# Four groups of small float32 matrix products taken in two halves of 64 weight columns

## The chip, the cores and the metric

The kernel runs on one core of a Trainium2 chip. A core has a matrix engine (TensorE, in the profile PE for its products and PEld for its weight loads), three engines for work on tiles (VectorE or DVE, ScalarE or ACT, GpSimd or POOL) and a queue processor, SyncE or SP, from which most transfers are issued. Matrix products read SBUF and write PSUM, which has eight banks. The metric is the device time of one execution in microseconds; the median of three runs before the change is 2164.58 us.

## The reference

One decoder layer over 4096 tokens of width 1024. The input is normalised and modulated to h; one projection of h feeds three groups of heads side by side. Their outputs are gated, joined, projected, normalised and added to the input.

```python
def _gla_mixer(h, q, k, v, gk1, gk2, gk_b, norm_w):
    gk = jax.nn.log_sigmoid(((h @ gk1) @ gk2 + gk_b).astype(f32)) / GLA_GATE_NORMALIZER
    ...
    def step(S, inp):
        b = jnp.cumsum(g_c, axis=2)
        A = jnp.einsum('bhid,bhjd,bhijd->bhij', q_c, k_c, jnp.exp(diff))
        o = A @ v_c + jnp.einsum('bhid,bhdv->bhiv', q_c * jnp.exp(b), S)
        S = ...
# in _rwkv7_mixer
    a = jax.nn.sigmoid((a0 + (xa @ a1) @ a2).astype(f32))
```

The groups are attention over a window of 128 tokens (8 heads), RWKV-7 (4 heads, a recurrence over tokens with a 64 by 64 state per head) and GLA (4 heads with 32 keys and 64 values each). The change touches four small products: the gate `(h @ gk1) @ gk2 + gk_b` of GLA, the scores `A` of GLA, the output `o` of GLA (scores by values plus queries by state), and `(xa @ a1) @ a2` of RWKV, called a-lora here.

## The kernel before

The work has two halves. The first goes through 16 steps of 256 tokens and computes h, its transpose (written to DRAM), the projections that RWKV and GLA need, and both recurrences, whose outputs go to DRAM. The second half does attention, the gates and the output projection. The change lies in the first half; the second half's program text is the same.

**Products and their shapes.** Large projections are float16 products with 128 by 128 weights and 256 moving columns. Small products are float32. A product with fewer than 128 weight rows or columns uses a part of the matrix engine: the code calls the pair (row quarters, column quarters) its mode. RWKV's products are already written for halves: `atp`, `rp`, `up` and one `yp` in mode (2, 2), that is 64 rows by 64 columns, `sp` and the other `yp` in mode (4, 2), 128 rows by 64 columns; parts of its triangular solve (`Xp`, `Xq`) have 32 by 32. The column half of a product is given by the PSUM partitions that it writes, 0 to 63 or 64 to 127.

**The stages of a step.** Each stage is a generator, and step i has eleven: among them `stage_a` (h and its transpose, `tp`), `stage_p` (projections `pv`, `lp`, `zz`, `gqk`), `stage_d` (the stream "w": GLA gate, decays, a-lora), `stage_r` (GLA), `stage_qa`, `stage_qb`, `stage_qc` (scores and triangular solve of RWKV, with a way through DRAM), `stage_k`, `stage_v` and `stage_q2` (the RWKV recurrence). The four groups of products are:

- `gp` in `gla_gate`, called from `stage_d`: 17 rows, 128 weight columns, 128 moving columns, twice per step. ACT (`ga`) and DVE (`gl`) read it.
- `aps` in `stage_d`: rows 64 to 127, 128 weight columns, 256 moving, twice per step; ACT (`ta`) reads it.
- `gap` in `stage_r`: for each of two blocks of 128 tokens (`a`) and each half of the heads (`hp`), 64 rows, 128 weight columns, 256 moving. The two halves lie in two PSUM banks, "at" and "mq". DVE masks them into `qb`.
- `op_` in `stage_r`: for each block, `qg` by the state `Gc` (128 rows, 128 weight columns, 256 moving), then per head the masked scores `qb` by values (64 moving columns), all summed in bank "at". ACT copies it to `osb`.

"at" has one buffer and is shared with `atp` of `stage_qa`; "mq" is shared by many.

**What sets the order.** The order of the instructions on each engine is not that of the program text. A first pass (`emit`, `Lane`) steps the generators by estimated times; there a float32 product counts 4 passes of its moving columns, and 0.55 of that if it writes at most 64 partitions. This gives each instruction a rank. A second pass (`Order.note`, `Order.pin`) lists every instruction with estimated durations, what it needs and which buffers it waits for, and then schedules all five engines, SP's and POOL's included, greedily by rank and fixes the order found. For PE it keeps a mode: a change of mode waits for the array to empty and costs 0.094 us in the estimate. While PE is in full mode (4, 4), a ready product of another mode is put off as long as full ones are ready, up to `TILING_WAIT`, 0.6 us; while PE is in another mode it goes on with that mode as long as anything of it is ready:

```python
if e == "PE" and mode is not None and steps[k].array[0] != mode:
    same = [q for q in at if steps[q].array[0] == mode]
    wait = max(now - ready[e][q] for q in at if steps[q].array[0] != mode)
    if same and (mode != (4, 4) or wait < TILING_WAIT):
        k = same[0]
```

The estimate of a float32 product's issue is 0.007 us a pass in mode (4, 4), 0.009 with one row quarter, 0.16 in mode (2, 4), 0.03 otherwise; its length is two passes of two cycles per moving column, at least 0.109 us a pass if it uses all columns.

The profile's line L320 is the helper that records every instruction, so groups are told apart by tile names.

Of the kernel before, what the change touches and what calls it, by code (L numbers as in the profile page):

```python
# [21 lines left out]
P = 128  # L22
D = 1024
T = 4096
NT = 256
# [358 lines left out]
def hybrid_kernel(ctx, tc, x, vecs, rows, adaw, w1, wl, w2, wo, w2aug, a2, gk2, cst, ctr, ctg, abias, out):  # L384
# [5 lines left out]
    PE = Lane(model, nc.tensor, *LANES[3], serial=True)  # L390
# [189 lines left out]
    def gla_gate(vg, zlT, ga, gl, tile_of):  # L580
        zp = tile_of("zp")
        for a in range(2):
            PE.transpose(zp[:17, a * P : (a + 1) * P], vg[:, a, 256:273], ident)
        V.tensor_copy(zlT, zp[:17, :NT])
        yield [zlT, "m"]
        gp = tile_of("gp")
        for a in range(2):
            PE.matmul(gp[:, a * P : (a + 1) * P], zlT[:, a * P : (a + 1) * P], gk2s, start=True, stop=True)
        S.activation(ga, gp[:, :NT], AF.Abs)
        S.activation(ga, ga, AF.Exp, scale=-1.0)  # L590
        S.activation(ga, ga, AF.Ln, bias=1.0)
        V.scalar_tensor_tensor(gl, gp[:, :NT], 0.0, ga, op0=ALU.min, op1=ALU.subtract)
# [31 lines left out]
    with ExitStack() as p1:  # L624
# [18 lines left out]
        def cs2(shape, name, dt=F32):  # L643
            return wt(shape, name, 2, dt, "c2")
# [36 lines left out]
        a2s = pp.tile([P, 256], F32, name="a2s")  # L681
        nc.scalar.dma_start(a2s[64:128, :], a2)
        gk2s = cp.tile([17, 128], F32, name="gk2s")
# [92 lines left out]
        for n, cc in enumerate((4, 5, 0, 6, 7, 1, 2, 3)):  # L776
            if cc in PE_BLOCKS:
                for jj in range(2):
                    aw = half_tile().rearrange("p (k c) -> p k c", k=KD)
                    SP.dma_start(aw, adaw[cc, :, :, jj * P : (jj + 1) * P])  # L780
                    for k in range(KD):
                        PE.matmul(adp[:, 2 * cc + jj : 2 * cc + jj + 1], aw[:, k, :], scol[:, k : k + 1], start=(k == 0),
                                  stop=(k == KD - 1))
# [25 lines left out]
        hp = mt("hp")  # L809
# [292 lines left out]
        def stage_d(i):  # L1102

            e = E[i]
            yield [("vg", i), ("w", i - 1)]
            vg = e["vg"]
            yield [vg, "m"]
            gl = wt([P, NT], "gl", 1)
            yield from gla_gate(vg, b1([17, NT], "zlT"), b1([P, NT], "ga"), gl, mt)
            yield [gl, "m"]  # L1110
            cgp = mt("cgp")
            for a in range(2):
                PE.matmul(cgp[:, a * 129 : (a + 1) * 129], gl[:, a * P : (a + 1) * P], CTG, start=True, stop=True)
            egp = wt([P, 2, 129], "egp", 2)
            egm = wt([P, 2, 129], "egm", 2)
            e["egp"], e["egm"] = egp, egm
            cg3 = cgp[:, :258].rearrange("p (a n) -> p a n", a=2)
            cgc = wt([P, 2, 129], "cgc", tag="gl")
            V.tensor_scalar(cgc, cg3, -40.0, 40.0, op0=ALU.max, op1=ALU.min)
            gm2 = st.tile([P, 2], F32, tag="gm2", name="gm2")  # L1120
            V.tensor_reduce(gm2, cg3[:, :, 0:129:128].rearrange("p a n -> p n a"), axis=AX.X, op=ALU.max)
            V.tensor_tensor(gmax, gmax, gm2[:, 0:1], op=ALU.max)
            V.tensor_reduce(gm2, cg3[:, :, 0:129:128].rearrange("p a n -> p n a"), axis=AX.X, op=ALU.min)
            V.scalar_tensor_tensor(gmax, gm2[:, 1:2], -1.0, gmax, op0=ALU.mult, op1=ALU.max)
            S.activation(egp, cgc, AF.Exp)
            S.activation(egm, cgc, AF.Exp, scale=-1.0)
            yield [("x1", i)]
            x1 = e["x1"]
            yield [x1]
            S.activation(uw[0:64, :], x1[0:64, :], AF.Tanh)  # L1130
            yield [uw, ("z", i - 1), "m"]
            wps = mt("wps")
            for a in range(2):
                PE.matmul(wps[:, a * NT : (a + 1) * NT], uw[:, a * P : (a + 1) * P], w2s, start=True, stop=True)
            gw = wt([P, 2, NT], "gw")
            S.activation(gw, wps.rearrange("p (a n) -> p a n", a=2), AF.Tanh, scale=0.5)
            V.tensor_scalar(gw, gw, 1.0, -0.5 * EM05, op0=ALU.add, op1=ALU.mult)
            yield [gw, "m"]
            ep = wt([P, 2, 4, 65], "ep", 1)
            em = wt([P, 2, 4, 65], "em", 1)  # L1140
            e["ep"], e["em"] = ep, em
            for b in range(2):
                cw = mt("cw")
                for a in range(2):
                    PE.matmul(cw[:, a * 130 : (a + 1) * 130], gw[:, a, b * P : (b + 1) * P], CT, start=True, stop=True)
                S.activation(ep[:, b].rearrange("p c n -> p (c n)"), cw[:, :260], AF.Exp)
                S.activation(em[:, b].rearrange("p c n -> p (c n)"), cw[:, :260], AF.Exp, scale=-1.0)
                yield ["m"]
            aps = mt("aps")
            for b in range(2):  # L1150
                PE.matmul(aps[:, b * NT : (b + 1) * NT], a2s[64:128, b * P : (b + 1) * P], x1[64:128, :],
                          start=True, stop=True)
            ta = wt([P, 2, NT], "ta")
            e["ta"] = ta
            for b in range(2):
                S.activation(ta[:, b, :], aps[:, b * NT : (b + 1) * NT], AF.Tanh, scale=0.5, bias=a0h[:, b : b + 1])
            yield [("q2", i - 2)]

            cd = wt([P, 2, 4], "cd", 2)
            em0 = wt([P, 2, 1], "em0", 2)  # L1160
            e["cd"], e["em0"] = cd, em0
            V.tensor_mul(cd[:, :, 0:3], ep[:, :, 0:3, 64], em[:, :, 1:4, 0])
            V.tensor_copy(cd[:, :, 3:4], ep[:, :, 3, 64:65])
            V.tensor_copy(em0, em[:, :, 0, 0:1])
# [174 lines left out]
        def stage_r(i):  # L1339

            e = E[i]
            yield [("p", i), ("r", i - 1)]
            qg, kg, vg, egp, egm = e["qg"], e["kg"], e["vg"], e["egp"], e["egm"]
            qb = [cs2([P, 4, P], "qb") for _ in range(2)]
            for a in range(2):
                G.tensor_tensor(qb[a], qg[:, a, :].rearrange("p (o n) -> p o n", o=1).to_broadcast([P, 4, P]),
                                bdm.rearrange("p (h n) -> p h n", h=4)[:, :, 0:1].to_broadcast([P, 4, P]), op=ALU.mult)
            yield [kg, "mq"]
            ktp = mq("ktp")
            for a in range(2):  # L1350
                PE.transpose(ktp[:, a * P : (a + 1) * P], kg[:, a, :], ident)
            kt = wt([P, 2, P], "kt", 1)
            S.copy(kt.rearrange("p a n -> p (a n)"), ktp[:, :NT])
            for a in range(2):
                yield [qb[a], "at", "mq"]
                gap = [pst(tag, "gap")[:, 0:NT] for tag in ("at", "mq")]
                for hp in range(2):
                    sl = slice(64 * hp, 64 * hp + 64)
                    PE.matmul(gap[hp], kg[sl, a, :], qb[a][sl, 2 * hp : 2 * hp + 2, :].rearrange("p h n -> p (h n)"),
                              start=True, stop=True)  # L1360

                for hp in range(2):
                    V.tensor_tensor(qb[a][:, 2 * hp : 2 * hp + 2, :], gap[hp].rearrange("p (h n) -> p h n", h=2),
                                    gmask.rearrange("p (o n) -> p o n", o=1).to_broadcast([P, 2, P]), op=ALU.mult)
            yield [kt, "mq"]
            osb = wt([P, 2, NT], "osb", 1)
            for a in range(2):
                gidx = 2 * i + a
                Gc, Gn = Gst[gidx % 2], Gst[(gidx + 1) % 2]
                if gidx > 0:  # L1370
                    V.tensor_scalar(Gc, Gc, egm[:, a, 0:1], None, op0=ALU.mult)
                kvp = mq("kvp")
                PE.matmul(kvp[:, :NT], kt[:, a, :], vg[:, a, 0:256], start=True, stop=True)
                V.tensor_tensor(Gn, kvp[:, :NT], Gc, op=ALU.add)
                V.scalar_tensor_tensor(Gn, Gn, egp[:, a, 128:129], bdm, op0=ALU.mult, op1=ALU.mult)
                yield [Gc, qb[a], "at"]
                op_ = pst("at", "op")
                PE.matmul(op_[:, :NT], qg[:, a, :], Gc, start=True, stop=False)
                for h in range(4):
                    PE.matmul(op_[:, h * 64 : h * 64 + 64], qb[a][:, h, :], vg[:, a, h * 64 : h * 64 + 64],  # L1380
                              start=False, stop=(h == 3))
                S.copy(osb[:, a, :], op_[:, :NT])
                yield [Gn, "mq"]
            osq = cs2([P, 2, NT], "osq")
            gla_norm(osb, osq)
            yield [osb, "mq"]

            gla_mix(osb, osb, mq("ot"))
            SP.dma_start(mscr[i][:, 2 * NT : 4 * NT], osb.rearrange("p b n -> p (b n)"))
# [513 lines left out]
    vg = fxt[:, 0:546].rearrange("p (a n) -> p a n", a=2)  # L1903
# [148 lines left out]
```

## Time and profile before

| what | value |
|---|---|
| three runs | 2167.91, 2161.32, 2164.58 us; median 2164.58 |
| span of the profiled execution, first to last instruction | 2148.0 us |
| the profiled execution as a whole | listed by its span alone; the median of the runs lies 16.6 us above it |
| mean granted clock of TensorE | 0.988 |
| busy: PE, weight loads, DVE, ACT, POOL | 2037.3, 1600.4, 1626.2, 1144.5, 199.9 us |
| products and weight loads on PE | 23735 each |
| the first half's busy stage | about 60 to 1060 us |
| the second half | from about 1120 us |

Busy time of an engine is the time covered by its instructions; what PE's instructions cover includes modelled ends that overlap the next start. The queries used are the busy time by stretches of the span, the groups of instructions kept apart by shape (count, busy us, mean ns of one, idle time before them and what ended it), all instructions of one tile, and the timeline, in which neighbours of one kind are merged into one row. In a shape such as 64*128 the first number is the weight rows, the second the weight columns.

### The profile page before, as it was taken

Reading aid. Unit: us, or ns where it says so; the run is one execution under the profiler, and the core shown is the slowest. Engines: PE = TensorE matmul, PEld = TensorE weight load, DVE = VectorE, ACT = ScalarE, POOL = GpSimd, SP = SyncE. Lnnn points to the kernel's source line nnn. Section 1 sums busy time; section 2 is a strip of 40 time slices with the busy share of each in tenths; the row PEclk is TensorE's granted clock in tenths of the full one; section 3 lists DMA queues with packets and bytes.
Section 4 is the critical chain, followed back from the end, with each engine's and each line's share of the span. In section 5 each row is a group of like instructions: output and inputs, shape, how many; then the busy total and the mean of one; then the engine's idle time right before and its main releaser. Section 6 shows DMA issues by size and latency. Waiting matters only on the chain. (4 is left out here: it accounts for less than half of the span.)

```text
span 2148.0 us, 59214 instructions
## 1 busy us (share of the span) xinstructions
PE 2037.3 (95%) x23735; PEld 1600.4 (75%) x23735; DVE 1626.2 (76%) x5204; ACT 1144.5 (53%) x2741; POOL 199.9 (9%) x404
## 2 busy tenths in 40 slices
PE   4999999999999999999878999999999999999996
PEld 4778878888888887777657667777777777777773
DVE  6677677787777689887756888777778877777876
ACT  3966666667676667754324444434344444444442
POOL 0011111110111110112700000000000000000000
PEclk9999999999999999999989999999999999999998
DMA  9232322232323134422515343433343333334341
GB/s 316 91 108 82 93 77 84 71 96 84 120 78 107 42 108 123 126 83 62 172 53 179 128 160 106 135 103 111 115 135 121 121 121 111 115 115 141 110 132 69
DMA packets 187243, 241.80 MB, mean 113 GB/s; under 512 B 52160, under 2 KB 145874, under 8 KB 182740
## 3 DMA queue, kind: packets, MB, share of 16 engines
q1 hardware_dynamic: 185220, 236.76, 34.1%
q8 instruction: 188, 3.08, 0.6%
q10 hardware_dynamic: 1744, 1.21, 0.2%
q14 instruction: 91, 0.75, 0.1%
HBM read 177.08 MB, written 60.82 MB: 111 GB/s over the span
## 5 line engine op out<-in xcount | busy, mean ns | idle before, releaser
L320 PEld LDWEIGHTS <-mtp 128*128 128x128 f16 x1344 | 130.7, 98 | 143.9 <-issue 5.1
L320 PE MATMUL op<-o,mtp 128*128 128x512 f16 x768 | 174.2, 380 | 0.0
L320 ACT ACTIVATE pr<-pr,nm,lsc 128x256 f32<-128x256 f32 (+1 forms) x256 | 149.2, 585 | 38.6 <-DVE nm L320 38.6
L320 PE MATMUL op<-ov,mtp 128*128 128x512 f16 x576 | 146.0, 384 | 2.1 <-ACT mtp L320 2.1
L320 PEld LDWEIGHTS <-hT 128*128 128x128 f16 x1536 | 117.4, 99 | 22.9 <-issue 4.4
L320 DVE TENSOR_TENSOR yv<-op,yv 128x512 f32<-128x512 f32 x112 | 75.2, 683 | 57.6 <-PE op L320 40.6
L320 DVE CUSTOM_DVE_ANT_0 pr<-sc,ab,sinks 128x256 f32<-128x256 f32 (+1 forms) x256 | 108.1, 476 | 13.3 <-PE sc L320 8.4
L320 ACT ACTIVATE mtp<-yv,oi 128x1024 f16<-128x1024 f32 x32 | 36.6, 1144 | 126.3 <-DVE yv L320 124.8
L320 ACT ACTIVATE ag<-gp,gh 128x512 f32<-128x512 f32 x64 | 43.7, 682 | 108.2 <-PE gp L320 108.2
L320 PE MATMUL pv<-gvh,hT 128*128 128x272 f16 x512 | 99.8, 284 | 1.4 <-DVE kg L320 1.3
L320 DVE SCALAR_TENSOR_TENSOR ag<-ag,gp 128x512 f32<-128x512 f32 x64 | 43.8, 684 | 71.4 <-ACT ag L320 71.3
L320 POOL COPY kT<-kT 128x512 f16<-128x512 f16 x15 | 9.8, 652 | 896.5 <-DVE kT L320 896.5
L320 PE MATMUL zz<-hT,kh 128*128 128x256 f16 x512 | 92.7, 273 | 0.0
L320 PE MATMUL qp<-hT,q1h 128*128 128x256 f16 x512 | 88.9, 277 | 2.7 <-issue 2.3
L320 PE MATMUL gqk<-hT,gqkh 128*128 128x256 f16 x512 | 87.5, 273 | 4.0 <-DVE zb L320 3.3
L320 PE MATMUL zz<-hT,rh 128*128 128x256 f16 x512 | 89.5, 278 | 0.0
L320 PE MATMUL lp<-hT,Lh 128*128 128x256 f16 x512 | 89.3, 273 | 0.1
L320 PE MATMUL qp<-hT,q0h 128*128 128x256 f16 x512 | 85.4, 273 | 2.7 <-DVE ag L320 2.3
L320 PE MATMUL zz<-hT,vh 128*128 128x256 f16 x512 | 87.8, 273 | 0.0
L320 PE MATMUL gp<-hT,q3h 128*128 128x256 f16 x512 | 87.2, 276 | 0.1
L320 PE MATMUL gp<-hT,q5h 128*128 128x256 f16 x512 | 86.7, 273 | 0.0
L320 ACT ACT_TABLE_LOAD x65 | 83.4, 1283 | 5.3 <-DMA sinks<-in_rows 4.2
(428 smaller groups left out, 6146.8 us busy)
## 6 DMA issues: line engine op xcount, KB each, us to landing
ov<-woscr SPq DMA_DIRECT2D x96, 512.0 KB, 4.1
xt<-in_x SPq DMA_DIRECT2D x16, 1024.0 KB, 4.9
hscr<-hT SPq DMA_DIRECT2D x16, 1024.0 KB, 4.7
hT<-hscr SPq DMA_DIRECT2D x16, 1024.0 KB, 4.9
out<-yv SPq DMA_DIRECT2D x32, 512.0 KB, 2.9
x<-in_x SPq DMA_DIRECT2D x30, 512.0 KB, 3.9
cs<-in_w SPq DMA_DIRECT2D x112, 128.0 KB, 2.2
v<-vscr SPq DMA_DIRECT2D x128, 64.0 KB, 3.0
```

What stands on the lines that cost most here:

```text
L320: r = f(*args, **kw)
```

## The change

Every product of the four groups is issued twice, each time with 64 of the 128 weight columns, writing PSUM partitions 0 to 63 and 64 to 127 of the same bank. The moving operand is the same for both. The arithmetic, the tiles and the readers stay as they are. The modes become: `gp` (1, 4) to (1, 2), `aps` and `gap` (2, 4) to (2, 2), `op_` (4, 4) to (4, 2). In `gap` the loop over column halves is the outer one, in the others the inner one. `gla_gate` is also used by a fallback that runs only for extreme gates and isn't entered here. Since the second pass lists instructions with their modes, the order on all engines in the first half is computed anew.

```diff
         gp = tile_of("gp")
         for a in range(2):
-            PE.matmul(gp[:, a * P : (a + 1) * P], zlT[:, a * P : (a + 1) * P], gk2s, start=True, stop=True)
+            for h in range(2):
+                PE.matmul(gp[64 * h : 64 * h + 64, a * P : (a + 1) * P], zlT[:, a * P + 64 * h : a * P + 64 * h + 64], gk2s,
+                          start=True, stop=True)
...
             for b in range(2):
-                PE.matmul(aps[:, b * NT : (b + 1) * NT], a2s[64:128, b * P : (b + 1) * P], x1[64:128, :],
-                          start=True, stop=True)
+                for h in range(2):
+                    PE.matmul(aps[64 * h : 64 * h + 64, b * NT : (b + 1) * NT],
+                              a2s[64:128, b * P + 64 * h : b * P + 64 * h + 64], x1[64:128, :], start=True, stop=True)
...
+            half = (slice(0, 64), slice(64, 128))
...
-                for hp in range(2):
-                    sl = slice(64 * hp, 64 * hp + 64)
-                    PE.matmul(gap[hp], kg[sl, a, :], qb[a][sl, 2 * hp : 2 * hp + 2, :].rearrange("p h n -> p (h n)"),
-                              start=True, stop=True)
+                for hk in half:
+                    for hp, sl in enumerate(half):
+                        PE.matmul(gap[hp][hk], kg[sl, a, hk], qb[a][sl, 2 * hp : 2 * hp + 2, :].rearrange("p h n -> p (h n)"),
+                                  start=True, stop=True)
...
-                PE.matmul(op_[:, :NT], qg[:, a, :], Gc, start=True, stop=False)
+                for ht in half:
+                    PE.matmul(op_[ht, :NT], qg[:, a, ht], Gc, start=True, stop=False)
                 for h in range(4):
-                    PE.matmul(op_[:, h * 64 : h * 64 + 64], qb[a][:, h, :], vg[:, a, h * 64 : h * 64 + 64],
-                              start=False, stop=(h == 3))
+                    for ht in half:
+                        PE.matmul(op_[ht, h * 64 : h * 64 + 64], qb[a][:, h, ht], vg[:, a, h * 64 : h * 64 + 64],
+                                  start=False, stop=(h == 3))
```

## The prediction

> **What bounds the kernel now.** I read the page's engine table first, then busy time by stage, then the groups of PE instructions kept apart by shape, then PE's timeline around the four groups that change.
>
> ```profile
> span 2148.0 us, 59214 instructions
> PE 2037.3 (95%) x23735; PEld 1600.4 (75%) x23735; DVE 1626.2 (76%) x5204; ACT 1144.5 (53%) x2741; POOL 199.9 (9%) x404
> ```
>
> The busy times by stage (columns: PE, PEld, DVE, ACT, POOL, granted clock, DMA share, GB/s):
>
> ```profile
> 60.00:1060.00 1000.00, 972.47 (x12921) 800.61 (x12918) 764.37 (x2724) 658.05 (x1520) 172.94 (x348) 0.99 0.31 94
> 1120.00:2148.00 1028.00, 986.93 (x9994) 738.06 (x9991) 783.43 (x2178) 446.00 (x1132) 9.16 (x14) 0.99 0.37 122
> ```
>
> ```profile
> 800.00:850.00 50.00, 46.66 (x497) 38.56 (x493) 44.95 (x176) 39.05 (x88) 6.76 (x15) 1.00 0.43 129
> 850.00:900.00 50.00, 49.11 (x703) 39.06 (x701) 44.86 (x170) 33.49 (x77) 6.98 (x16) 1.00 0.40 117
> 900.00:950.00 50.00, 48.84 (x700) 39.37 (x699) 43.41 (x125) 33.44 (x73) 9.06 (x16) 1.00 0.34 107
> ```
>
> Everything that is edited runs in the first half, up to about 1060 us. There PE is without work for 27.5 us of 1000, at a clock of 0.99, and the next engine, DVE, has 764. So PE bounds this half, and time that a product gives back on PE is worth nearly its full length. The exception is 800 to 950 us, where DVE is busy for 133 of 150 us; there I count half. That makes 0.85 + 0.15/2 = 0.925 of what PE saves.
>
> A busy PE says little about its inside: modelled ends overlap the next start. So I price products by start-to-start distances, not by busy time. The groups of the change are
>
> ```profile
> L320 PE MATMUL op<-vg,qb 128*128 128x64 f32 x256 | 33.1, 269 | 0.0
> L320 PE MATMUL gap<-qb,kg 64*128 64x256 f32 x128 | 29.3, 428 | 0.3 <-DVE AT L320 0.3
> L320 PE MATMUL op<-Gst,qg 128*128 128x256 f32 x64 | 20.0, 394 | 1.1 <-DVE Gst L320 1.1
> L320 PE MATMUL aps<-x,a2s 64*128 64x256 f32 x64 | 17.9, 400 | 0.2
> L320 PE MATMUL gp<-gk2s,zlT 17*128 17x128 f32 x64 | 11.8, 306 | 0.0
> ```
>
> "64*128" is the part of the array used, rows by columns. The counts are twice the products in the code: a float32 product is two passes, each with a weight load.
>
> **The price of a change of shape.** PE's timeline (start, duration of the merged run, what, how many passes):
>
> ```profile
> 943.35 0.70 PE L320 MATMUL gap<-qb,kg 64*128 64x256 f32 x2
> 943.98 0.39 PE L320 MATMUL zz<-hT,kh 128*128 128x256 f16 x2
> ...
> 258.89 1.13 PE L320 MATMUL aps<-x,a2s 64*128 64x256 f32 x4
> 259.95 0.39 PE L320 MATMUL zz<-hT,kh 128*128 128x256 f16 x2
> ...
> 812.05 0.70 PE L320 MATMUL gap<-qb,kg 64*128 64x256 f32 x4
> 812.59 1.02 PE L320 MATMUL aps<-x,a2s 64*128 64x256 f32 x4
> 813.54 0.45 PE L320 MATMUL sp<-UV,BK 128*64 128x64 f32 x8
> ```
>
> At 812.59 four passes follow a product of the same shape and take 0.95 us to the next start; at 258.89 the same four come behind another shape and take 1.06: the difference, 0.11, is a first weight load that nothing covers. Two passes of gap take 0.63 (943.35 to 943.98), four of aps 1.06: two passes cost 0.43, so a pass 0.215, and 0.63 - 0.43 - 0.11 leaves 0.09 for emptying the array before another shape may enter. At 812.05 four gap passes take no longer (0.54, no change of shape behind) than two would: the two row halves run side by side. So each change of shape costs 0.09, and the first load behind it 0.11 with 128 columns.
>
> What a load of 64 columns costs (shortest, median, longest duration in ns; first and last start), with the first and last op, for a count below:
>
> ```profile
> L320 PEld LDWEIGHTS gap<-qb,kg x128: 182/184/186, 123.0 to 1063.4; 64*128 64x128 f32 x128
> L320 PEld LDWEIGHTS aps<-x,a2s x64: 182/187/187, 97.8 to 1013.5; 64*128 64x128 f32 x64
> L320 PEld LDWEIGHTS sp<-UV,BK x512: 132/138/232, 172.6 to 1117.3; 128*64 128x64 f32 x171
> ...
> L320 PE MATMUL op<-Gst,qg x64: 377/379/483, 129.8 to 1068.9; 128*128 128x256 f32 x64
> ```
>
> The median falls from 184-187 to 138 ns, so 0.05 less: 0.06.
>
> **Part 1: op (32 per run, 16 steps by 2).** Now, within full-shape work:
>
> ```profile
> 502.81 0.27 PE L320 MATMUL zz<-hT,kl 128*128 128x256 f16 x1
> 502.92 0.60 PE L320 MATMUL op<-Gst,qg 128*128 128x256 f32 x2
> 503.35 1.00 PE L320 MATMUL op<-vg,qb 128*128 128x64 f32 x8
> 504.19 0.61 PE L320 MATMUL tp<-ident,xt 128*128 128x128 f32 x4
> ```
>
> 1.27 us: 0.43 for the state product, 0.84 for the eight passes of 64 moving columns, which are 0.105 apart, the length of a load of 128 columns and not of the stream. Split in column halves, op has the shape 128*64 of sp and yp:
>
> ```profile
> 697.88 0.45 PE L320 MATMUL sp<-UV,BK 128*64 128x64 f32 x8
> 698.17 0.40 PE L320 MATMUL yp<-UV,AT 128*64 128x64 f32 x8
> 698.50 0.39 PE L320 MATMUL zz<-hT,kh 128*128 128x256 f16 x2
> ```
>
> Sixteen half passes in 0.62 us; less 0.09 and a first load of 0.06 that is 0.47, or 0.058 for a pair of halves. The eight passes then cost 0.46 instead of 0.84: 0.38 x 32 = 12.2 us less. The state product stays at 0.43 if its halves of 256 columns run side by side, which no row shows at that length (rival 2).
>
> But op leaves the shape of the projections between which it runs today. Following PE's order from the first op at 129.8 us to the last at 1068.9, I count 38 unbroken runs: 11 lie between full-shape work (two new changes each), 19 have a tiled shape other than 128*64 on one side (one new each), 8 touch sp or yp (none). That is 41 x 0.09 = 3.7 us. First loads: 25 runs that begin behind full-shape work get an open one of 0.06, 9 behind another tiled shape pay 0.06 instead of 0.11, 4 behind 128*64 lose 0.11: +0.6. Op: 12.2 - 3.7 - 0.6 = 7.9 us gained. Bounds: every run a visit of its own, 38 x (0.18 + 0.06 + 0.01 for the projection's reload) = 9.5, gain 2.7; all next to sp or yp, gain 12.2. I take the counted neighbours, since the rule that orders the work stays.
>
> **Parts 2 and 3: gap and aps** go from 64*128 to 64*64, the shape of atp, rp, up. Streaming stays at 0.43 for a pair of row halves and 0.86 for aps. In the order I count 57 visits to 64*128 between 97.8 and 1063.6 us. Each saves 0.05 of its first load: 2.9. At 21 of their ends the neighbour is 64*64 already; there the change (0.09) and an open load (0.06) go: 3.1. Together 6.0; bounds 2.9 (nothing adjoins) and 57 x (0.18 + 0.11) = 16.5 (all merge).
>
> **Part 4: gp**, 16 visits from 17*128 to 17*64.
>
> ```profile
> 236.83 0.71 PE L320 MATMUL gp<-gk2s,zlT 17*128 17x128 f32 x4
> 237.47 0.39 PE L320 MATMUL lp<-hT,Lh 128*128 128x256 f16 x2
> ```
>
> 0.64 less 0.09 and 0.11 leaves four passes of 0.11, stream and load alike; only the first load shrinks: 16 x 0.05 = 0.8, at worst 0.
>
> **What else moves.** 36 more passes and loads per step, 576 in all; they start behind one another, priced above. DVE, ACT and POOL get no instruction more or less. ACT's copy of op (osb) comes earlier by what op gains and later by what it waits for the change of shape, up to the planner's 0.6 us; behind it stand the norm and the release of PSUM bank "at", for which gap, atp and the next op queue. I cost that at nothing, since the projections cover it on PE; without that cover it is rival 4. The planner rewrites the order of all five engines, SP's and POOL's queues among them, because its prices for these products change; I have no row for that and take 0, with about 6 us to either side.
>
> **Sum.** 7.9 + 6.0 + 0.8 = 14.7 us on PE, x 0.925 = 13.6, from a span of 2148.0 to 2134.4. The median of the runs, 2164.58, lies 16.6 above that span; I leave that share as it is: 2164.6 - 13.6 = 2151. Bounds: (2.7 + 2.9) x 0.925 = 5 and (12.2 + 16.5 + 0.8) x 0.925 = 27, so 2137 to 2160.
>
> **Rivals.**
> 1. *The gain is handed on.* PE ends its products sooner, and what it then needs is no earlier: DVE at 764 of 1000 and the recurrence set the pace, or op's runs scatter so that the lower bounds hold. For it: the 150 us with DVE at 89%; against: 27.5 us idle in 1000 today. Gain 0 to 6: about 2161, no change.
> 2. *The halves of 256 columns do not run side by side.* Then streaming doubles for the state product (0.43 x 32), gap (0.43 x 41 visits), aps (0.86 x 16) and gp (0.43 x 16): 52 us, less 14.7, x 0.925: 2199. Against it:
>
> ```profile
> 300.98 1.10 PE L320 MATMUL atp<-RA,KB 64*64 64x128 f32 x32
> 301.91 0.33 PE L320 MATMUL rp<-UV,AT 64*64 64x64 f32 x5
> ```
>
> 32 passes of 128 columns in 0.93 us: four at a time in 0.11, as long as one of gp. At 256 columns it would have to fail anew; it decides once a pair takes over 0.28 instead of 0.215 (52 x 0.3 = 15.6). [...]
> [...]
> 4. *Slower: op at the gate holds bank "at".* As a tiled product op must wait for PE to change shape. If its state product and its four others are taken in two visits, "at" stays closed between them, atp comes late, and with it the solve that goes through DRAM and the recurrence behind it. It decides at (13.6 + 6.5) / 32 = 0.63 us of uncovered PE time per op; at 0.8 us it gives 2151 + 25 = 2176. For it: 10 of the 38 runs hold only part of an op already. Against: today's 27.5 us of idle time for all causes.
>
> **Chances.** Forecast 0.60 (2138 to 2158 by itself); rival 1 0.20; rival 2 0.05; rival 3 0.02; rival 4 or another loss in the rewritten order 0.13. What a measurement can tell here from no change is 0.3%, 6.5 us. So faster 0.60, same 0.22 (rivals 1 and 3), slower 0.18 (2 and 4). Range 2138 to 2172: the low end is just inside the bound of all merging, the high end reaches into rival 4 and leaves out 2.
>
> **What would show it.** op's passes 128*64, pairs 0.058 apart, 1.27 us falling to 0.9 plus the change of shape; aps still 0.86 between first and last pass; no 64*128 left; 128*64 visits up by about 30; PE's idle time in 60 to 1060 us still under 40 us and that stage ending some 13 us sooner; the half from 1120 us on as long as before. I am wrong if pairs of 256 columns start 0.43 apart, if the stage ends as late with PE waiting more for DVE or ACT, or if op falls apart into far more than 38 runs.

## The result, and the profile after

The changed kernel takes 2149.89 us, the median of four executions (2148.88 to 2150.68); the kernel before took 2166.24 beside it. The ratio is 0.9931, with a 95% interval of 0.9911 to 0.9951. Measured again on another chip (run after_again) it is 0.9928 [0.9910, 0.9947]: 13 to 16 us, or 0.7%, are gained.

The profile page of the changed kernel begins (engine, busy us, share, instructions):

```profile
span 2148.7 us, 60377 instructions
PE 2025.3 (94%) x24311; PEld 1577.1 (73%) x24311; DVE 1630.7 (76%) x5204; ACT 1142.8 (53%) x2739; POOL 203.5 (9%) x404
```

Its span is that of the profiled execution before, 2148.0 us, within 1 us. Laid side by side the two first traces show no gain at all, because that execution of the kernel before was an unusually short one: another trace of it (before_again) spans 2164.1 us. Experiments 1 and 5 show what the difference between two executions consists of. Two executions on record, one of 5073 us (of less_pe_new_order, experiment 4) and one of 2353 us (of the kernel before, beside experiments 3 and 4), lie far off all others and are left out of the ratios.

Busy time by stage of the changed kernel (PE, PEld, DVE, ACT, POOL, granted clock, DMA share, GB/s):

```profile
60.00:1060.00 1000.00, 959.33 (x13468) 777.85 (x13469) 768.88 (x2724) 653.87 (x1514) 175.14 (x346) 0.99 0.31 94
1120.00:2148.00 1028.00, 984.38 (x9945) 734.57 (x9942) 781.42 (x2168) 446.32 (x1131) 9.25 (x14) 0.99 0.37 122
```

and of the kernel before in its typical execution:

```profile
60.00:1060.00 1000.00, 968.80 (x12805) 796.74 (x12803) 762.73 (x2718) 655.43 (x1513) 170.74 (x342) 0.99 0.31 94
1120.00:2148.00 1028.00, 998.51 (x10176) 747.34 (x10173) 778.81 (x2170) 446.16 (x1136) 9.12 (x14) 0.99 0.38 121
```

PE does its products of the first half in less time and stands idle longer: 40.7 us of 1000 where it was 31.2. Work that PE saves and then idles away is no gain by itself; this was the first sign that the prediction's reason was not the whole of it.

The products themselves came out close to their prices. Their groups (busy us, mean ns of one, then idle time before them):

```profile
L320 PE MATMUL gap<-qb,kg 64*64 64x256 f32 x256 | 37.5, 392 | 0.3 <-ACT kt L320 0.3
L320 PE MATMUL op<-vg,qb 128*64 128x64 f32 x512 | 22.9, 222 | 0.0
L320 PE MATMUL op<-Gst,qg 128*64 128x256 f32 x128 | 20.5, 391 | 1.3 <-DVE Gst L320 1.3
L320 PE MATMUL aps<-x,a2s 64*64 64x256 f32 x128 | 18.4, 385 | 0.1
```

and one op of the changed kernel in PE's timeline (start, duration, what, passes):

```profile
504.15 0.40 PE L320 MATMUL yp<-UV,AT 128*64 128x64 f32 x8
504.38 0.60 PE L320 MATMUL op<-Gst,qg 128*64 128x256 f32 x4
504.82 0.63 PE L320 MATMUL op<-vg,qb 128*64 128x64 f32 x16
505.38 0.38 PE L320 MATMUL wssp<-wss,ones 128*128 128x1 f32 x2
```

The four half passes of the state product take 0.44 us to the next start, where two whole ones took 0.43: halves of 256 columns run side by side. The sixteen half passes take 0.56, of which 0.09 is the change of shape at their end: 0.47, where eight whole passes took 0.84. The op stands in one visit with yp, so it begins without a change of shape.

### The profile page after: what moved, and what is told of

Its sections match the earlier page's. It is cut to its first block, busy times and chain, and to the rows that moved or that the text cites. A ratio compares the mean times of both kernels' runs of the same rounds, so it can differ in the third digit from the quotient of the medians.

```text
span 2148.7 us, 60377 instructions
## 1 busy us (share of the span) xinstructions
PE 2025.3 (94%) x24311; PEld 1577.1 (73%) x24311; DVE 1630.7 (76%) x5204; ACT 1142.8 (53%) x2739; POOL 203.5 (9%) x404
## 5 line engine op out<-in xcount | busy, mean ns | idle before, releaser
L320 PE MATMUL gp<-hT,q4h 128*128 128x256 f16 x512 | 85.0, 273 | 0.0
```

The lines of the kernel that those rows point to most:

```text
L320: r = f(*args, **kw)
```

## The experiments

Every instruction of the first half is listed in a planner, whose second pass fixes the order of all engines. In some kernels below the planner is given one product and the program another, so that the order stays while the products change, or the reverse.

### 1. Both kernels again

No edit.

> The kernel before, unchanged. The page of before has a span of 2148.0 us and that of the changed kernel 2148.7, although the timed medians are 2166.2 and 2149.9. Theory A (PE's shorter products pass through to the end): the profiled execution of before was an unusually short one; this kernel comes out at 2161 to 2169 again, and a new trace of it has a span of about 2160. Theory C (the gain is no property of the products but of which executions were timed): executions of about 2150 turn up here too and the median lies below 2160.

> The changed kernel, unchanged. Theory A: 2149 to 2152, ratio to before 0.992 to 0.995. Theory C: a ratio between 0.997 and 1.003.

Measured: 2164.89 us against 2163.22 for the other runs of the same kernel (1.0001 [0.9989, 1.0014]), and 2150.05 (0.9928 [0.9910, 0.9947]). The result stands.

The trace of before_again has the instructions of the first trace in the same order, so each VectorE instruction can be set against itself. Its lag behind the first trace is no slope but a staircase: -0.4 us at 785 us, +3.9 us across a stretch of 6.8 us at a granted clock of 0.5 (from 814 us), +9.6 us across one of 20.5 us (from 1050 us), then 4.0 between 1141 and 1218 us, where this trace has three of 3.4 us and the first one of 6.8 us; 16.2 us from there to the end. So 13.5 of the 16.2 us lie at two such stretches, at about half a microsecond for each microsecond of half clock. The rest are shifts of up to 1.6 us of both signs and the last 4.0, of which the 3.4 us more at half clock would be some 1.7. This is how the long one begins in before_again (PE first, clock after the engines):

```profile
1042.78:1046.20 3.42, 2.49 (x100) 2.03 (x97) 3.26 (x5) 0.12 (x1) 3.18 (x5) 1.00 0.60 203
1046.20:1049.61 3.41, 1.73 (x7) 0.54 (x7) 3.41 (x4) 0.00 (x0) 3.41 (x3) 1.00 0.64 185
1049.61:1070.09 20.48, 20.48 (x202) 15.19 (x203) 7.95 (x18) 0.52 (x2) 10.11 (x17) 0.50 0.33 115
```

and the same place in the first trace of the same kernel:

```profile
1040.31:1043.73 3.42, 2.10 (x75) 1.16 (x61) 3.42 (x5) 0.00 (x0) 3.42 (x3) 1.00 0.70 205
1043.73:1047.14 3.41, 2.35 (x23) 1.63 (x23) 3.41 (x8) 0.00 (x0) 1.30 (x4) 1.00 0.92 341
1049.61:1070.09 20.48, 19.42 (x280) 14.72 (x279) 12.76 (x37) 3.68 (x12) 16.03 (x25) 1.00 0.28 76
```

The hole in PE's work, 2.4 and 2.6 us in which it waits for the chain of the last step, is nearly the same. In one execution it falls into one interval of 3.41 us, of which PE is busy 1.73, and the clock halves; in the other it is shared by two intervals with 2.10 and 2.35, and the clock stays at 1.00. In the first traces of both kernels every change of the granted clock stands a multiple of 3.41 us from the others (their stretches at 0.50 up to 2120 us take 3.41, 6.83 or 13.65 us), and the intervals above are laid out from such changes. In before_again PE is, by the profile, busy for all of the 20.48 us, and the clock stays at 0.50 throughout.

### 2. The halves and the order, each alone

halves_old_order issues the four groups in halves, while the planner lists them whole, so that all five engines keep the order of the kernel before (in the trace they do up to 1085 us; from there to 1158 us some twenty instructions each of VectorE and ScalarE change places with neighbours):

```diff
+    def mm2(o, w, m, start, stop):
+        two = [nc.tensor.matmul(o[h : h + 64], w[:, h : h + 64], m, start=start, stop=stop) for h in (0, 64)]
+        model.order.made, model.order.twin[two[0].ins.name] = two[0], two[1].ins
+        PE.matmul(o, w, m, start=start, stop=stop)
+        model.order.made = None
...
-                PE.matmul(op_[:, :NT], qg[:, a, :], Gc, start=True, stop=False)
+                mm2(op_[:, :NT], qg[:, a, :], Gc, start=True, stop=False)
```

whole_new_order does the reverse: the planner lists halves, the program holds the whole product where the first half would stand.

```diff
+                model.order.made = nc.tensor.matmul(op_[:, :NT], qg[:, a, :], Gc, start=True, stop=False)
                 for ht in half:
                     PE.matmul(op_[ht, :NT], qg[:, a, ht], Gc, start=True, stop=False)
```

> The products are issued in halves as in the changed kernel, but the planner lists each pair of halves as the one whole product of before, so that all engines keep the order of before. Theory A, by the neighbours counted in the order of before: 13.6 us less than before, about 2152. Theory B (the gain lies in the new order, not in the products): within 4 us of before. Rival 1 of the prediction (lower bounds): 5 us less.

> The products are whole as in before, but stand where the changed kernel has their first halves, in its order on all engines. Theory A: a whole op between sp and yp now costs two changes of shape more and a whole gap or aps inside a run of 64*64 products up to two, so about 5 us for op and 8 us for gap and aps: 2172 to 2182, slower than before. Theory B: as fast as the changed kernel, about 2152.

Measured: 2162.95 us (0.9997 [0.9982, 1.0013]) and 2162.61 us (1.0000 [0.9981, 1.0019]). Neither gains anything: halves_old_order fits its theory B, and whole_new_order fits neither of its theories, which said 2172 to 2182 and 2152. The halves are no gain in the old order, and the new order is none with whole products. Only both together are.

In the old order the halves save as much on PE as elsewhere: busy time in 60 to 985 us falls from 901.14 (before_again) to 892.10:

```profile
60.00:985.00 925.00, 892.10 (x12415) 722.03 (x12416) 711.08 (x2567) 627.41 (x1452) 136.11 (x291) 1.00 0.30 91
```

and in before_again:

```profile
60.00:985.00 925.00, 901.14 (x11871) 743.61 (x11870) 708.50 (x2563) 627.50 (x1453) 136.09 (x288) 0.99 0.30 91
```

What PE saves it idles away. The trace shows one difference in how the halves stand. In the new order op shares its visit with sp or yp in 24 of 32 places, in the old one in 7, and PE changes shape 806 times in the whole program against 784 before; the changed kernel does so 740 times. The 22 changes more at 0.09 us are 2 us, too little to explain the rest.

### 3. Op alone and the others alone, each replanned

op_only makes the edit in op alone, others_only the one in gap, aps and gp; both are planned anew.

```diff
-                PE.matmul(op_[:, :NT], qg[:, a, :], Gc, start=True, stop=False)
+                for ht in half:
+                    PE.matmul(op_[ht, :NT], qg[:, a, ht], Gc, start=True, stop=False)
```

> Only op is issued in halves; gap, aps and gp are whole; the planner orders anew. Theory A (each group gives what its products save on PE, as the prediction priced them): 7.9 us x 0.925 = 7 us less, about 2156. Theory D (a new order decides, whatever products bring it about): any value from -15 to +5 us, not ordered by what the products save. Together with the next run the two parts add up to -13 under theory A.

> Only gap, aps and gp are issued in halves; op is whole; the planner orders anew. Theory A: 6.8 us x 0.925 = 6 us less, about 2157. Theory D: as above, and the sum of the two runs differs from -13 by more than 5 us.

Measured: 2164.49 (1.0016 [1.0001, 1.0032]) and 2163.73 us (1.0012 [0.9997, 1.0027]). Each part with the order that the planner makes for it is worth nothing or a little less, so theory A fails, and the gain is no sum over parts while the order moves too. In op_only the planner's order has op in one visit with sp or yp in 24 of 32 places, just as in the changed kernel, and its halves still gain nothing.

### 4. Less work on PE without the change

In both orders 128 products of the low weight half for lp in the odd steps are left out of the program (the result lacks that part of lp); the planner still lists them. By the trace this takes some 9 us of PE's busy time out of the first half in the old order, and by the estimate in the expectation 14 us of its work (128 x 0.109; in the first trace of before lp's products start 0.109 us apart, the median).

```diff
-                yield from proj(lp[:, b * NT : (b + 1) * NT], Wt["L"], b * P, P, hT)
+                yield from proj(lp[:, b * NT : (b + 1) * NT], Wt["L"], b * P, P, hT, i % 2)
```

> The kernel before, in its own order, without 128 of lp's products (those with the low half of the weights, in every second step): this leaves out 14 us of PE work (128 x 0.109) spread over the first half and computes lp with the rounded weights alone there; the planner still lists them, so that no other instruction moves. Theory A (PE bounds the first half): 13 us less, about 2150. Rival 1 of the prediction (in this order the gain is handed on to waits): 0 to 5 us less; the halves in the old order, which gave 0.3 us, are then explained by that alone.

> The same 128 products left out of the changed kernel, in its own order. If the new order is one in which PE bounds and the old one is not: 13 us less than the changed kernel, about 2137, and clearly more than the old order gives. If both orders hand the gain on: 0 to 5 us less, about 2147.

Measured: 2164.02 us (1.0005 [0.9986, 1.0024]) in the old order and 2149.89 (0.9932 [0.9916, 0.9949]) in the new one, the time of the changed kernel. Both times the case without a bound on PE holds: less work on PE gains nothing that these runs can tell in either order (the intervals are 0.2% to each side, the expected 13 us are 0.6%). The first row is less_pe_new_order, the second after_again:

```profile
60.00:985.00 925.00, 885.43 (x12240) 716.37 (x12240) 714.11 (x2567) 624.31 (x1453) 138.95 (x288) 0.99 0.30 92
60.00:985.00 925.00, 892.41 (x12295) 724.06 (x12292) 709.28 (x2558) 623.88 (x1451) 138.69 (x288) 0.99 0.30 91
```

In less_pe_new_order PE is busy 885 of 925 us; the changed kernel has 892 there and ends at the same time. So PE's work does not bound this half, in spite of a busy share of 97%. What a single product is worth that the step waits for is another question (experiment 6).

### 5. The clock in the turn between the halves

dense_fill is the kernel before with 18 extra dense products that nobody reads, in the hole near 1045 us:

```diff
+                fill = [nc.tensor.matmul(gp2[:, 0:256], ones.bitcast(BF16)[:, 0:P], ones.bitcast(BF16), start=True, stop=True).ins
+                        for _ in range(18 if g == 0 else 0)]
-                PE.matmul(gp2, ones, acc.rearrange("p n c -> p (n c)"), start=True, stop=True)
+                r = PE.matmul(gp2, ones, acc.rearrange("p n c -> p (n c)"), start=True, stop=True)
+                model.order.fill[r.ins.name] = fill
```

Behind the fill a few products of the second half move by some places among those of the chain; these are not planned, and the first qp comes no earlier for it. VectorE and ScalarE have the same changes of place there as in halves_old_order, which gains nothing.

> The kernel before with 18 extra products of ones with ones (16 bit, 128 x 256, nobody reads them), all placed ahead of the first of the two products gp<-acc, near 1045 us, where the traces of this order show TensorE idle for 1.7 to 2.6 us inside 3.4 us. Their own time is an estimate from 256 columns of 16 bit at 0.108 us each: 1.9 us. Theory A, the clock: in this order the granted clock falls to 0.5 for 17 us or more near 1050 us in most executions, because of that hole, and this is the time that the changed kernel saves: with the hole filled no stretch at 0.5 over 7 us between 1040 and 1075 us, and 2152 us (2149 to 2156), 10 us under the kernel before. Theory B, the chain of the last step through VectorE sets the turn and the low clock only goes with it: the stretch goes and the time stays at 2163, or rises by the 2 us to 2165.

> The whole products standing in the order of the changed kernel once more, for a second trace: its profiled execution was 2152.2 us long, its median 2162.6 us. Theory A: an execution near the median shows a stretch of 14 us or more at a granted clock of 0.5 between 1000 and 1120 us, and one under 2155 us shows none. Theory B: an execution near the median shows the same stretches as the short one, and its 8 to 10 us lie in waits spread over the first half.

Measured, dense_fill: 2157.75 us (0.9978 [0.9959, 0.9997]). Added work makes the kernel faster, by 5 us, less than theory A said (2149 to 2156) and more than B. The twelve executions fall into two groups: eight from 2152.9 to 2158.0 us with mean granted clocks of 0.984 to 0.989, four from 2163.2 to 2167.2 with 0.978 to 0.982. The profile caught one of the four:

```profile
1046.01:1049.42 3.41, 3.41 (x52) 2.52 (x44) 3.41 (x3) 0.00 (x0) 3.41 (x3) 1.00 0.56 143
1049.42:1052.83 3.41, 2.24 (x49) 1.58 (x48) 3.41 (x8) 0.00 (x0) 1.30 (x4) 1.00 0.97 320
1052.83:1069.90 17.07, 17.07 (x164) 12.65 (x158) 6.00 (x13) 0.52 (x2) 8.58 (x14) 0.50 0.26 83
```

Here 1.2 us is left of the hole, and the clock halved behind it all the same. So half of theory A fits: the stretch near 1050 us costs the kernel before time, and the fill seems to remove it in most executions. That the two groups differ by this stretch rests on one trace and the clocks, no more.

Measured, whole_new_again: 2166.26 us (1.0011 [0.9986, 1.0037]); its profiled execution spans 2162.9 us. Theory A fails here. There is no long stretch in the turn: the longest is 6.8 us, and the lag behind the first, short trace of that kernel grows by steps at 79, 362, 929 and 977 us, each at a stretch of 3.4 to 6.8 us, to 9.0 us at 986 us and 9.6 at 1218. So the clock explains how executions of one kernel differ, in whichever place; it does not explain the gain. For that the traces have to be compared at equal clock. The tables below take half of the time at a clock of 0.5, by the clock record of each trace and from 62 us on, off the start of the last pv, a product of the last step's projections, and then off the span:

| trace | last pv starts, us | at half clock before it, us | at equal clock, us |
|---|---|---|---|
| old order, whole: before / before_again / dense_fill | 984.4 / 988.9 / 988.0 | 6.8 / 10.2 / 10.2 | 981.0 / 983.8 / 982.9 |
| old order, whole, less lp | 989.7 | 10.2 | 984.6 |
| old order, halves | 986.2 | 6.8 | 982.8 |
| new order, whole: both traces | 982.5 / 991.5 | 3.4 / 20.5 | 980.8 / 981.3 |
| new order, halves: after / after_again | 979.6 / 984.3 | 17.1 / 27.3 | 971.1 / 970.7 |
| new order, halves, less lp | 979.2 | 20.5 | 969.0 |

| trace | span, us | at half clock from 62 to 1215 us | span at equal clock |
|---|---|---|---|
| old order, whole: before / before_again / dense_fill | 2148.0 / 2164.1 / 2163.5 | 34.1 / 58.0 / 58.0 | 2131 / 2135 / 2134 |
| old order, halves | 2162.2 | 61.4 | 2132 |
| new order, whole: both traces | 2152.2 / 2162.9 | 27.3 / 47.8 | 2139 / 2139 |
| new order, halves: after / after_again | 2148.7 / 2150.5 | 47.8 / 54.6 | 2125 / 2123 |

The factor of one half is an estimate, from the steps of experiment 1 (0.47 to 0.57 of a stretch for the two that fall into dense work). With it two traces of one kernel, 16 and 11 us apart, come within 4 us and 1 us. By these traces the new order with whole products is level with the old one at the last pv (981 against 981 to 984) and some 5 us worse at the end; in it the halves gain 10 us by the last pv and 14 to 16 us by the end. In the old order they gain nothing. In the steady steps the changed kernel spends more time at half clock, 17 and 27 us against 7 and 10; PE also idles more there.

A kernel has one or two traces, and a span and a mean clock of every execution. The span times the mean clock is the span less half of its time at half clock, over the whole program:

| executions | number | mean of span times clock, us (95%) |
|---|---|---|
| old order, whole, beside all experiments | 101 | 2124.3 ± 1.1 |
| old order, halves | 12 | 2122.8 ± 3.1 |
| new order, whole | 19 | 2124.1 ± 3.1 |
| new order, halves (the changed kernel) | 10 | 2114.4 ± 2.5 |
| new order, op alone in halves (experiment 6) | 12 | 2113.6 ± 3.6 |
| new order, the others alone in halves (experiment 6) | 12 | 2123.8 ± 2.2 |

By this measure the order by itself costs nothing, and the halves gain 10 us in it. The 5 us of the traces are no more than two executions of one kernel can differ by. The measure counts half clock ahead of 62 us too, where the 20.5 us of before_again cost 0.5 us, and such stretches add to its spread.

### 6. Which product it is

All engines in the new order, in one kernel only op in halves, in the other only gap, aps and gp.

```diff
-                model.order.made = nc.tensor.matmul(op_[:, :NT], qg[:, a, :], Gc, start=True, stop=False)
                 for ht in half:
                     PE.matmul(op_[ht, :NT], qg[:, a, ht], Gc, start=True, stop=False)
```

> All engines in the order of the changed kernel; only op in halves, gap, aps and gp whole, each standing where its first half stood. In this order all whole gave 2162.6 and 2166.3 us, all halves 2150 us, so the halves are worth some 13 to 15 us here. Theory A (the prediction's sizes hold in this order, since each product stands on the path of the step): the parts add, op's 7.9 x 0.925 = 7.3 us, 2156 us (2153 to 2159). Theory B (one product bears it all, because only its length is on that path): 2150 to 2152 if it is op, 2162 to 2166 if it is not. Theory C (only all together move the path): over 2160.

> The counterpart: all engines in the order of the changed kernel; gap, aps and gp in halves, op whole. Theory A: the prediction's 6.8 x 0.925 = 6.3 us, 2157 us (2154 to 2160). Theory B: 2150 to 2152 if gap, aps and gp bear it all, 2162 to 2166 if op does. Theory C: over 2160.

Measured: op alone 2148.26 us (0.9954 [0.9936, 0.9972], the kernel before 2160.33 beside it), the others alone 2159.09 (0.9997 [0.9980, 1.0014]). Op bears most of it, so theory B is nearest, though both kernels, and the kernel before beside them, read 3 us lower than it said. By its ratio op alone gains 6 to 14 us, which the 7.3 of theory A is just in; the 6.3 us that A gives the others are outside their interval. What is between op alone and all four (0.9928) is not told apart from nothing, since the intervals overlap. In the traces the last pv starts at equal clock at 971.5 us with op in halves (976.6, 10.2 us at half clock) and at 975.4 with the others (982.2, 13.7), where all whole has 981 and all halves 971. So this one trace would give the others 6 us, which neither their ratio nor the mean over their executions (experiment 5) bears out. Last pv of op_halves_new_order and of op_whole_new_order (shortest, median, longest ns; first to last start):

```profile
L320 PE MATMUL pv<-gvh,hT x512: 279/279/434, 56.0 to 976.6; 128*128 128x272 f16 x171
```

```profile
L320 PE MATMUL pv<-gvh,hT x512: 279/279/434, 55.5 to 982.2; 128*128 128x272 f16 x171
```

PE's busy time does not follow the gain: 60 to 985 us it is 899.66 with op in halves,

```profile
60.00:985.00 925.00, 899.66 (x12209) 735.51 (x12209) 716.90 (x2569) 627.11 (x1456) 138.89 (x288) 0.99 0.30 91
```

and 896.70 with the others, which gain nothing that the runs can tell:

```profile
60.00:985.00 925.00, 896.70 (x12031) 736.54 (x12030) 712.28 (x2563) 624.59 (x1452) 137.25 (x288) 0.99 0.30 91
```

This fits a product being worth what it adds to the chain that the step waits on, and not what it adds to PE; no trace was followed along that chain.

A second piece of the gain lies outside the steady steps. The kernels with op whole in the new order lose 4 to 5 us between about 1096 and 1120 us against those with op in halves, in each of nine pairs of traces. whole_new_again has there, in PE's timeline,

```profile
1110.93 0.38 PE L320 MATMUL X<-tc,Xs 32*32 32x32 f32 x12
1113.51 0.74 PE L320 MATMUL X<-tc,Xs 32*32 32x32 f32 x20 [2.21 <-issue]
1114.19 0.39 PE L320 MATMUL gp<-hT,q3h 128*128 128x256 f16 x1
```

a pause of 2.21 us in the midst of 32 small products that wait for nothing the profile shows, and behind it 6.8 us at half clock. In after_again the same 32 products run through:

```profile
1100.95 0.69 PE L320 MATMUL X<-tc,Xs 32*32 32x32 f32 x32
```

The pause is 2.4, 2.2 and 3.5 us in the three traces with op whole in the new order, at the same instruction of X. The traces show a regular place for such pauses: numbered over all instructions that a trace records for PE (products, weight loads and some 380 for semaphores), each of the 24 pauses of over 0.5 us that wait for nothing shown ("issue"), between 60 and 1120 us in the fourteen traces, stands 193 or 194 behind a multiple of 256 (ahead of the one of 2.27 us in the first trace of before stand 27330, 106 x 256 + 194); five of 0.9 us behind 1120 us stand elsewhere. Of some 110 such places in a trace, one to four show a pause. Halves of gap, aps and gp add 512 instructions ahead of it, twice 256, and leave the pause at its place in X; halves of op add 640, two and a half times 256, and move it. What PE waits for there the traces do not show, and no run changed the number of instructions alone. So this piece of the gain seems to come from where op's products put the later instructions in that count, not from a shorter op.

## Why the prediction was right and where it was wrong

The time was right (2151 against 2149.9), and the prices of the products nearly so. The reason given for why that price reaches the end was not.

- **"So PE bounds this half", factor 0.925: wrong, the step that failed.** Products of lp left out, 14 us of PE's work, gain nothing in either order (1.0005; 0.9932 against 0.9928), and the halves, which save 9 us of busy time in the old order, gain nothing there. The busy time that goes comes back as idle time: of 925 us PE idles 23.9 in before_again, 32.9 with the halves in the old order and 33.1 with less of lp. What the saving is worth depends on the order at hand; that it counts where the product stands on the chain of the step is the reading that fits, not shown. That 13.6 us came out is luck: op alone, priced at 7.3, gives some 10 us (0.9954; 2113.6 against 2124.3 at equal clock), the others, priced at 6.3, nothing, and a part may lie at the pause in the turn, which the prediction did not know (2.27 and 1.66 us in the two traces of before, 0.72 and none in those of the changed kernel).
- **Op, 1.27 to 0.89 us, and its changes of shape: the price right, the changes too dear.** Op measures 0.91 without the change of shape. Summed start to start over 60 to 1000 us (28 of the 32 ops), op went from 37.6 us in the first trace of before to 29.3 in after_again; that is 9.5 us for all 32, between the 7.9 that was taken and the bound of 12.2. The 41 new changes of shape did not come, because the planner moved op beside sp and yp: 740 changes in all against 784. The assumption that failed is that the neighbours stay. Where they do stay, in halves_old_order, the count was right: 806, 22 more, where the prediction's 41 less 21 give 20.
- **Gap and aps 6.0, gp 0.8: about right on PE, nothing in time that the runs can tell.** All visits to 64*128 are gone. With the order held (whole_new_again against op_whole_new_order) gap falls from 29.0 to 25.2 us and aps from 16.0 to 13.4 start to start, over 60 to 1000 us; gp saves about 1 us, less surely. Against the first trace of before, aps fell from 16.5 to 13.3, and gap did not fall (23.0 to 25.2), with waits in it. Alone, in the new order, the three give 0.9997.
- **"The planner rewrites the order ... and take 0, with about 6 us to either side": the size right, the role wrong.** With whole products the order gives 1.0000 and 1.0011, nothing by itself; and it is the condition for all of the gain.
- **Rival 1, the gain is handed on: it held in four kernels** (halves in the old order, each part replanned, and the others alone in the new order) and failed in two, the one that was asked for and op alone in its order. The prediction named the waits; it did not see that the order decides which of the two happens.
- **Rival 2: refuted.** Pairs of 256 columns take 0.22 us. **Rival 3**, a fixed issue time of each half pass: no run shows such a term; the sixteen half passes of 64 columns take 0.47 us, 0.03 each. **Rival 4:** no kernel ended later than before by more than 0.2%; op did fall into 51 unbroken runs instead of 38 (50 in the second trace), without harm, since sp and yp, of the same shape, stand between them: 36 visits to that shape hold them all.
- **Signs.** PE's idle time in 60 to 1060 us was to stay under 40 us; it is 40.7. The stage was to end 13 us sooner; typical traces show 4.6 at the last pv (988.9 to 984.3) and the rest in the turn up to 1215 us. The second half from there on is as long as before: the lag of whole_new_again behind after_again stays at 11.5 us from 1218 to 2108 us.
- **The span as the base of the sum.** The 16.6 us between span and median were carried along as a constant. They were not: in the other traces an execution lies about 2 us above its span (2165.91 and 2164.1 in before_again), and by the rest the profiled execution was a short one, mostly for the clock's sake (experiment 1). It did no harm, because only the difference was used.

Left open: why op's length counts in the new order and not in the old. That op stands beside yp and ahead of sp, on the recurrence, in the one and apart from it in the other fits the traces of these two orders. But op_only has it there as often (directly ahead of sp 12 times in both) and gains nothing, so this neighbourhood alone is not the reason. No run moved op alone.

## What to carry to other kernels

A busy share of 97% on PE is no proof that PE bounds: take a few per cent of its work out with the order held, and see whether the end moves, before pricing a change in PE time. Where a planner writes the order, test the change and the new order apart (products in the old order, old products in the new), since either may be worth nothing alone. Compare traces of two kernels only after the stretches at low clock are taken off each, for one such stretch of 20 us (9.6 us of time in experiment 1) is as large as a gain of half a per cent; and take the clocks and spans of all executions before believing a few microseconds from one trace of each.

## What the runs showed of the hardware

- The granted clock halved behind an interval of 3.41 us in which PE was busy for 0.00 us (first trace of the changed kernel, from 958.85 us), 1.73 (before_again, from 1046.20) or 2.24 (dense_fill, from 1049.42), and PE's busy time alone does not decide it: behind 2.10 of 3.42 in the first trace of before (from 1040.31 us) it did not, nor behind 1.57 of 3.42 (from 1074.45). It stayed halved for 3.41 us (first trace of before, from 1023.25 us) up to 20.48 us (before_again, with PE busy throughout, 20.48 of 20.48 us). Each microsecond of it cost 0.47 and 0.57 us in the two stretches that were followed, where PE had work; ahead of 62 us, 20.5 us of it cost 0.5.
- Added idle work shortened the kernel before: with 18 unread products its ratio is 0.9978 [0.9959, 0.9997].
- Halves of a float32 product with 64 weight columns run side by side: a pair of 256 moving columns in 0.22 us (0.44 for two pairs), a pair of 64 in 0.06 (0.47 for eight).
- PE paused for 0.5 to 3.5 us with nothing to wait for that the profile shows, often among products of 32x32 (all three pauses of the first trace of the changed kernel: 1.60, 0.86 and 0.72 us). In the first half all 24 such pauses stand 193 or 194 behind a multiple of 256 in the count of PE's instructions (weight loads and semaphore instructions counted): 512 more instructions ahead left the pause at its place in X, 640 moved it.
